# Attention slots that also fix the order of VectorE, ScalarE and GpSimd

## The chip, the cores and the metric

The kernel runs on one core of a Trainium2 chip. The metric is the device time in microseconds (us) of one execution. PE is TensorE's matmul stream and PEld its weight loads, DVE is VectorE, ACT ScalarE, POOL GpSimd, SP the queue that issues most DMAs.

## What is computed

One layer with three branches over 2048 tokens. The change touches only the first, the forgetting attention with 12 heads of 64 channels:

```
F = cumsum(log_f)                                     # per head
s = einsum('bhqd,bhkd->bhqk', q / 8, k)
s = s + F[query] - F[key];  s = where(key <= query, s, -1e30)
y = softmax(s) @ v;         y_fox = y * silu(gf)
```

The other branches (a state-space layer with a gated unit, an attention into 256 memory tokens), the projections, the gated merge and the final norm are as they were.

## The kernel before

The kernel has three parts. Until about 1587 us the input projections and the other two branches run. From there to about 2842 us the attention runs, with other matmuls mixed in ("fill"). Then the rest of the merge and the output follow. The change is in the middle part alone.

**Tasks and slots.** A task is one head `h` and one block `c` of 512 queries. There are 48: twelve heads with c=3, then with c=2, c=1 and c=0. A task with block c has 4(c+1) slots, one for each block of 128 keys: 16, 12, 8 and 4. In a slot `fox_score` makes the scores of 128 keys by 512 queries with two matmuls into one of two buffers `psA`. ScalarE copies them with a bias into `T` (L749), and VectorE takes the running maximum over keys into `mx` (L757; the first slot L759). The last four slots of a task lie on the causal diagonal: there GpSimd first adds a mask to the copy in `T` (L751), and VectorE takes the maximum from `T` (L753) and not from `psA`, over 512, 384, 256 and 128 columns.

**After the scores.** The rest of a task is put into a table `due` by slot, counted as d from its last score slot, so that it runs under the slots of the next task. At d=2 the maximum is transposed on PE into `psB` and reduced to `nm` (L767), then widened on ScalarE into `xb` (L772). At d=4 PE transposes `xb` into `psM`, which has one buffer ("rows"). Then `fox_exp`, for groups of four key blocks: VectorE adds the negative maximum (L789, two key blocks in one instruction of 1024 columns; L794 on the diagonal), ScalarE takes the exponential (L790, L795), GpSimd adds up the denominator in `acc` (L797, L799). PE multiplies with the values into `psC` from d=9 (`fox_pv`). `fox_den` divides, and `fox_end` multiplies with the gate: VectorE L839, then GpSimd L840 over `oo`. `psB` has one buffer too, for the transposes of `mx`, the denominator and the last transposes.

**Fill.** Per slot 0.67 steps of other work are put behind the scores: first the last input projections (`gen_gl`), then part of the merge (`gen_merge0`). A step is mostly six matmuls into `psF`. This work brings splits of weights in two halves, on GpSimd (L931) and VectorE (L933). Its eight first merge steps, somewhere in c=2, have no matmul.

**What sets the order.** The framework's scheduler orders each engine's instructions by its own timeline, and each engine then runs them in that order. For PE the kernel chains the matmuls (`te`), so that PE's order is that of the source. On the other three engines the scheduler moves an instruction ahead as soon as it takes its inputs for ready.

Of the kernel before, what the change touches and what calls it, by code (L numbers as in the profile page):

```python
# [17 lines left out]
CW = 512  # L18
# [4 lines left out]
DH = 64  # L23
# [24 lines left out]
class Layer:  # L48
# [98 lines left out]
        self.te("matmul", out, a[1], b[0], start=False, stop=last)  # L147

    def te(self, op, *a, **k):

        f = getattr(self.nc.tensor, op)
        if not self.chain:
            return f(*a, **k)  # L153
        with self.tc.issue_after(self.pe.ins) if self.pe else nullcontext():
            self.pe = f(*a, **k)  # L155
# [576 lines left out]

    def fox_score(self, p, u, kt):

        nc, h, c = self.nc, u["h"], u["c"]
# [12 lines left out]
        self.te("matmul", ps[:, w:], kk[:, ks], q[1][:, w:], start=False, stop=True)  # L748
        nc.scalar.activation(t[:, a:], ps[:, a:], AF.Identity, bias=bias)  # L749
        if j >= 0:  # L750
            nc.gpsimd.tensor_add(t[:, a:a + 128], t[:, a:a + 128], self.mask)  # L751
            if kt:
                nc.vector.tensor_max(mx[:, a:], mx[:, a:], t[:, a:])  # L753
            else:
                nc.vector.tensor_copy(mx, t)
        elif kt:
            nc.vector.scalar_tensor_tensor(out=mx, in0=ps, scalar=bias, in1=mx, op0=ALU.add, op1=ALU.max)  # L757
        else:
            nc.vector.tensor_scalar(out=mx, in0=ps, scalar1=bias, scalar2=None, op0=ALU.add)  # L759

    def fox_max(self, p, u):

        pt = self.psB()
        for b in range(4):
            self.te("transpose", pt[:, b * 128:(b + 1) * 128], u["mx"][:, b * 128:(b + 1) * 128], self.ident)
        nm = p.tile([128, 4], F32, tag="nm", name="nm", bufs=2)
        self.nc.vector.reduce_max(nm, pt.rearrange("p (b k) -> p b k", b=4), axis=AX.X, negate=True)  # L767
        self.fox_wide(p, u, nm, 128)

    def fox_wide(self, p, u, x, n):  # L770
        u["x"] = p.tile([128, 4, 128], F32, tag="xb", name="xb", bufs=2)
        self.nc.scalar.activation(u["x"][:, :, :n], x.unsqueeze(2).to_broadcast([128, 4, n]), AF.Copy)  # L772

    def fox_rows(self, u, ps, n):

# [1 line left out]
            self.te("transpose", ps[:n, b * 128:(b + 1) * 128], u["x"][:, b, :n], self.ident)  # L777
        return ps

    def fox_exp(self, p, u, g, i):  # L780

        nc, c = self.nc, u["c"]
        tg = u["T"][g]
        if g == 0 and i == 0:
            u["acc"] = p.tile([128, CW], F32, tag="acc", name="acc", bufs=2)
        acc, m = u["acc"], u["m"]
        if g < c:
            t = tg[:, i:i + 2, :]
            nc.vector.tensor_add(t, m.unsqueeze(1).to_broadcast([128, 2, CW]), t)  # L789
            nc.scalar.activation(t, t, AF.Exp)  # L790
        for e in (i, i + 1):
            t, a = tg[:, e, :], 128 * e if g == c else 0
            if g == c:
                nc.vector.tensor_add(t[:, a:], m[:, a:], t[:, a:])  # L794
                nc.scalar.activation(t[:, a:], t[:, a:], AF.Exp)  # L795
            if g or e:
                nc.gpsimd.tensor_add(acc[:, a:], acc[:, a:], t[:, a:])  # L797
            else:
                nc.gpsimd.tensor_copy(acc, t)  # L799

    def fox_pv(self, u, g):

# [14 lines left out]
    def fox_den(self, p, u):  # L817

        nc, h, c = self.nc, u["h"], u["c"]
        u["gf"] = p.tile([DH, CW], F32, tag="gf", name="gf", bufs=2)  # L820
        nc.sync.dma_start(out=u["gf"], in_=self.s["gf"][h * DH:(h + 1) * DH, c * CW:(c + 1) * CW])
        pd = self.psB()
        for b in range(4):
            self.te("matmul", pd[:, b:b + 1], u["acc"][:, b * 128:(b + 1) * 128], self.ones, start=True, stop=True)
        rd = p.tile([128, 4], F32, tag="rd", name="rd", bufs=2)
        nc.vector.reciprocal(rd, pd[:, 0:4])
        self.fox_wide(p, u, rd, DH)
        o = u["o"] = p.tile([DH, CW], F32, tag="oo", name="oo", bufs=2)
        a = 128 if c == 0 else 0
        if a:  # L830
            nc.gpsimd.memset(o[:, 0:a], 0.0)
        nc.scalar.copy(o[:, a:], u["po"][64:128, a:])
        nc.vector.tensor_add(o, u["po"][0:64, :], o)

    def fox_end(self, p, u):
        nc, h, c = self.nc, u["h"], u["c"]
        rb = self.fox_rows(u, self.psB(), DH)
        gf, o = u["gf"], u["o"]
        nc.vector.scalar_tensor_tensor(out=gf, in0=rb[:DH, :], scalar=0.5, in1=gf, op0=ALU.mult, op1=ALU.mult)  # L839
        nc.gpsimd.tensor_mul(o, o, gf)  # L840
        nc.sync.dma_start(out=self.s["yx"][h * DH:(h + 1) * DH, c * CW:(c + 1) * CW], in_=o)
        self.done += 1

    def gen_fox(self):

        p, self.close_f = self.pool("fox", side="right")
        self.ones = p.tile([128, 1], F32, name="ones")
        self.nc.vector.memset(self.ones, 1.0)  # L850
        seq = [(h, c) for c in range(NC - 1, -1, -1) for h in range(H)]
        ld = {0: self.k0}
        due, slot = {}, 0

        def rows(u):
            u["m"] = self.fox_rows(u, self.psum("M"), 128)

        def run():
            for f in due.pop(slot, ()):
                f()  # L860
        for n, (h, c) in enumerate(seq):
            u = {"h": h, "c": c, "ld": ld.pop(n)}
# [340 lines left out]
```

## Time and profile before

| | us |
|---|---|
| median of 3 runs | 3224.64 (3223.2 to 3231.12) |
| profiled execution | 3224.58, span 3222.4 |
| busy in the span: PE / DVE / POOL / ACT | 2998.0 / 1942.0 / 1104.7 / 1035.0 |
| attention, 1587 to 2842: PE / DVE / POOL / ACT of 1255 | 1072.45 / 876.37 / 838.28 / 608.86 |

PE is busy nearly all the time outside of the attention. Inside it PE's own work is dense too, but there are gaps, and the granted clock of PE is 0.92 on the mean. A matmul's end is modelled, so the start of the next one is what tells the pace.

### The profile page before, as it was taken

Reading aid. Unit: us, or ns where it says so; the run is one execution under the profiler, and the core shown is the slowest. Engines: PE = TensorE matmul, PEld = TensorE weight load, DVE = VectorE, ACT = ScalarE, POOL = GpSimd, SP = SyncE. Lnnn points to the kernel's source line nnn. Section 1 sums busy time; section 2 is a strip of 40 time slices with the busy share of each in tenths; the row PEclk is TensorE's granted clock in tenths of the full one; section 3 lists DMA queues with packets and bytes.
Section 4 is the critical chain, followed back from the end, with each engine's and each line's share of the span. In section 5 each row is a group of like instructions: output and inputs, shape, how many; then the busy total and the mean of one; then the engine's idle time right before and its main releaser. Section 6 shows DMA issues by size and latency. Waiting matters only on the chain.

```text
span 3222.4 us, 41372 instructions
## 1 busy us (share of the span) xinstructions
PE 2998.0 (93%) x14096; PEld 2312.9 (72%) x14096; DVE 1942.0 (60%) x3975; ACT 1035.0 (32%) x1840; POOL 1104.7 (34%) x1214
## 2 busy tenths in 40 slices
PE   8999999999999999999988888898788888889999
PEld 7889877777777778888755555566456556667787
DVE  5321589989976643222265555666778887755444
ACT  5112111111122222222255445555445444332222
POOL 0110000000013321221155555566678877722200
PEclk9999999999999999999999888999899998899999
DMA  5342224333346553443533333333456656577543
GB/s 165 111 119 58 72 84 125 106 97 125 127 133 178 165 180 105 129 128 115 150 101 91 91 85 94 96 104 107 135 139 171 197 162 176 176 239 218 172 143 105
DMA packets 283595, 424.90 MB, mean 132 GB/s; under 512 B 108136, under 2 KB 129384, under 8 KB 281848
## 3 DMA queue, kind: packets, MB, share of 16 engines
q1 hardware_dynamic: 283096, 422.19, 44.6%
q8 instruction: 112, 1.84, 0.2%
q14 instruction: 99, 0.81, 0.1%
q10 hardware_dynamic: 288, 0.07, 0.0%
HBM read 287.53 MB, written 134.61 MB: 131 GB/s over the span
## 4 chain that ended last, share of the span: by engine, by line
PE 70%; DVE 11%; DMA 7%; POOL 5%; issue 5%; ACT 2%; SPq 0%; DVEq 0%; POOLq 0%; ACTq 0%
PE psA L153 21%; PE psF L153 20%; PE psF L155 9%; PE psA L155 5%; PE psC L153 4%; PE psC L155 3%; DVE T L789 3%; POOL acc L797 3%; PE psB L153 2%; PE psB L155 2%; DVE T L794 1%; DMA wraw<-in_w_out 1%; DVE mx L753 1%; DVE mx L757 1%; DVE wlo L933 1%
## 5 line engine op out<-in xcount | busy, mean ns | idle before, releaser
L797 POOL TENSOR_TENSOR acc<-acc,T 128x512 f32<-128x512 f32 (+3 forms) x432 | 497.2, 1151 | 23.2 <-ACT T L790 1.5
L749 ACT ACTIVATE T<-psA,nf 128x512 f32<-128x512 f32 x480 | 293.5, 623 | 475.7 <-PE psA L155 444.6
L931 POOL TENSOR_SCALAR whi<-wraw 128x1024 fp32r<-128x1024 f32 (+2 forms) x168 | 168.3, 1002 | 782.5 <-PE psA L153 445.9
L933 DVE TENSOR_TENSOR wlo<-wraw,whi 128x1024 fp32r<-128x1024 f32 (+2 forms) x184 | 232.7, 1266 | 242.6 <-POOL whi L931 215.1
L155 PE MATMUL psA<-qh,kk 128*128 128x512 f32 x480 | 215.7, 450 | 134.1 <-DVE mx L757 124.8
L153 PE MATMUL psA<-hl,whi 128*128 128x512 f32 (+1 forms) x816 | 323.5, 397 | 0.0
L153 PE MATMUL psA<-hh,whi 128*128 128x512 f32 (+1 forms) x816 | 321.4, 395 | 1.7 <-ACT hh L193 1.0
L153 PE MATMUL psA<-hh,wlo 128*128 128x512 f32 (+1 forms) x816 | 322.1, 395 | 0.6 <-DVE wlo L933 0.6
L153 PE MATMUL psF<-hh,whi 128*128 128x512 f32 (+1 forms) x776 | 308.4, 397 | 4.0 <-DVE elo L234 2.5
L153 PE MATMUL psF<-hh,wlo 128*128 128x512 f32 (+1 forms) x776 | 308.1, 397 | 0.1
L153 PE MATMUL psF<-hl,whi 128*128 128x512 f32 (+1 forms) x776 | 308.0, 397 | 0.0
L155 PEld LDWEIGHTS psA<-qh,kk 128*128 128x128 f32 x480 | 96.8, 202 | 240.2 <-DVE mx L757 154.9
L757 DVE SCALAR_TENSOR_TENSOR mx<-psA,nf,mx 128x512 f32<-128x512 f32 x252 | 188.3, 747 | 121.3 <-ACT T L749 115.8
L155 PE MATMUL psC<-T,v 128*64 128x512 f32 (+1 forms) x960 | 212.2, 544 | 0.0
L753 DVE TENSOR_TENSOR mx<-mx,T 128x384 f32<-128x384 f32 (+3 forms) x180 | 145.3, 807 | 100.2 <-POOL T L751 95.8
L155 PE MATMUL psA<-ql,kk 128*128 128x512 f32 x480 | 184.1, 385 | 0.0
L153 PEld LDWEIGHTS psA<-hh,whi 128*128 128x128 f32 x816 | 153.8, 189 | 37.1 <-POOL whi L931 1.8
L153 PEld LDWEIGHTS psA<-hh,wlo 128*128 128x128 f32 x816 | 154.4, 189 | 35.3 <-DVE wlo L933 0.8
L153 PEld LDWEIGHTS psA<-hl,whi 128*128 128x128 f32 x816 | 154.5, 189 | 33.7 <-issue 0.2
L155 PE MATMUL psF<-ymg,whi 128*128 128x512 f32 x512 | 175.8, 427 | 0.0
L153 PEld LDWEIGHTS psF<-hh,whi 128*128 128x128 f32 x776 | 146.6, 189 | 39.0 <-DVE elo L234 3.3
L789 DVE TENSOR_TENSOR T<-psM,T 128x1024 f32<-128x1024 f32 x144 | 166.4, 1216 | 13.0 <-PE psM L155 12.9
(360 smaller groups left out, 6477.2 us busy)
## 6 DMA issues: line engine op xcount, KB each, us to landing
wraw<-in_w_in SPq DMA_DIRECT2D x90, 512.0 KB, 4.0
s_gl<-ehi SPq DMA_DIRECT2D x96, 256.0 KB, 2.4
g<-s_gl SPq DMA_DIRECT2D x96, 256.0 KB, 4.6
wraw<-in_w_proj SPq DMA_DIRECT2D x48, 320.0 KB, 3.4
qh<-s_qh SPq DMA_DIRECT2D x96, 128.0 KB, 4.2
ql<-s_ql SPq DMA_DIRECT2D x96, 128.0 KB, 5.8
wraw<-in_w_glu SPq DMA_DIRECT2D x24, 384.0 KB, 4.6
x<-in_x SPq DMA_DIRECT2D x16, 512.0 KB, 4.5
```

The costliest lines, as they stand in the source:

```text
L153: return f(*a, **k)
L155: self.pe = f(*a, **k)
L749: nc.scalar.activation(t[:, a:], ps[:, a:], AF.Identity, bias=bias)
L753: nc.vector.tensor_max(mx[:, a:], mx[:, a:], t[:, a:])
L757: nc.vector.scalar_tensor_tensor(out=mx, in0=ps, scalar=bias, in1=mx, op0=ALU.add, op1=ALU.max)
L789: nc.vector.tensor_add(t, m.unsqueeze(1).to_broadcast([128, 2, CW]), t)
L794: nc.vector.tensor_add(t[:, a:], m[:, a:], t[:, a:])
L797: nc.gpsimd.tensor_add(acc[:, a:], acc[:, a:], t[:, a:])
L931: self.nc.gpsimd.tensor_scalar(out=hi, in0=x, scalar1=sc, scalar2=1.0, op0=ALU.mult, op1=ALU.mult)
L933: self.nc.vector.tensor_sub(lo, x, fl32(hi))
```

## The change

`te` becomes a case of `ch`, which chains the instructions of any engine in the order of the source, and the attention's instructions on VectorE, ScalarE and GpSimd all go through it (so they carry the one line L159 afterwards). The fill's instructions on these engines stay free. In the table the work of a slot is split into what comes before the score (order 0) and behind it (order 1). The subtractions become `fox_sub`, of which one pair of key blocks is due in every second slot, and the exponentials follow one slot later. The widening (`fox_wide`) and the division's second half (`fox_out`) get slots of their own. At each of the three changes of c four slots without a score are put in; fill runs there too.

```diff
+    def ch(self, eng, op, *a, **k):
+        f = getattr(getattr(self.nc, eng), op)
         if not self.chain:
             return f(*a, **k)
-        with self.tc.issue_after(self.pe.ins) if self.pe else nullcontext():
-            self.pe = f(*a, **k)
+        last = self.last.get(eng)
+        with self.tc.issue_after(last.ins) if last else nullcontext():
+            self.last[eng] = f(*a, **k)
...
-        nc.scalar.activation(t[:, a:], ps[:, a:], AF.Identity, bias=bias)
+        self.ch("scalar", "activation", t[:, a:], ps[:, a:], AF.Identity, bias=bias)
         if j >= 0:
-            nc.gpsimd.tensor_add(t[:, a:a + 128], t[:, a:a + 128], self.mask)
+            self.ch("gpsimd", "tensor_add", t[:, a:a + 128], t[:, a:a + 128], self.mask)
...
+    def fox_sub(self, u, g, i):
+        tg, m = u["T"][g], u["m"]
+        if g < u["c"]:
+            t = tg[:, i:i + 2, :]
+            self.ch("vector", "tensor_add", t, m.unsqueeze(1).to_broadcast([128, 2, CW]), t)
+        else:
+            for e in (i, i + 1):
+                self.ch("vector", "tensor_add", tg[:, e, 128 * e:], m[:, 128 * e:], tg[:, e, 128 * e:])
...
         for n, (h, c) in enumerate(seq):
             u = {"h": h, "c": c, "ld": ld.pop(n)}
+            for _ in range(4 if n and h == 0 else 0):
+                idle()
+                slot += 1
+                yield
             for kt in range(4 * (c + 1)):
-                run()
+                run(0)
                 self.fox_score(p, u, kt)
+                run(1)
...
-            at(1, self.fox_values, p, u)
-            at(2, self.fox_max, p, u)
-            at(4, rows, u)
+            at(1, 1, self.fox_values, p, u)
+            at(2, 1, self.fox_max, p, u)
+            at(3, 1, self.fox_wide, p, u, 128)
+            at(4, 0, rows, u)
             for g in range(c + 1):
                 for i in range(2):
-                    at(4 + 4 * g + 2 * i, self.fox_exp, p, u, g, 2 * i)
-                at(9 + 4 * g, self.fox_pv, u, g)
-            at(11 + 4 * c, self.fox_den, p, u)
-            at(13 + 4 * c, self.fox_end, p, u)
+                    at(4 + 4 * g + 2 * i, 1, self.fox_sub, u, g, 2 * i)
+                    at(5 + 4 * g + 2 * i, 1, self.fox_exp, p, u, g, 2 * i)
+                at(9 + 4 * g, 0, self.fox_pv, u, g)
+            at(11 + 4 * c, 1, self.fox_den, p, u)
+            at(12 + 4 * c, 1, self.fox_out, p, u)
+            at(13 + 4 * c, 1, self.fox_end, p, u)
```

What the table makes of the engines' orders shows at three places. The rows name an instruction by line, operation, output and inputs.

**VectorE, a task with c=3.** Before, from the first score of a task on (`mx<-psA` is the maximum of a score, `T<-psM,T` a subtraction of the task before):

```order
L759 TENSOR_SCALAR mx<-psA,nf 128x512
L767 TENSOR_REDUCE nm<-psB 128x4
L757 SCALAR_TENSOR_TENSOR mx<-psA,nf,mx 128x512 x2
L789 TENSOR_TENSOR T<-psM,T 128x1024 x6
L794 TENSOR_TENSOR T<-psM,T 128x512
L794 TENSOR_TENSOR T<-psM,T 128x384
L794 TENSOR_TENSOR T<-psM,T 128x256
L794 TENSOR_TENSOR T<-psM,T 128x128
L757 SCALAR_TENSOR_TENSOR mx<-psA,nf,mx 128x512
```

Now, over the diagonal of a task and the first two scores of the next one:

```order
L159 TENSOR_TENSOR T<-psM,T 128x1024
L159 TENSOR_TENSOR mx<-mx,T 128x512
L159 TENSOR_TENSOR mx<-mx,T 128x384
L159 TENSOR_TENSOR T<-psM,T 128x1024
L159 TENSOR_TENSOR mx<-mx,T 128x256
L159 TENSOR_TENSOR mx<-mx,T 128x128
L159 TENSOR_TENSOR T<-psM,T 128x512
L159 TENSOR_TENSOR T<-psM,T 128x384
L159 TENSOR_SCALAR mx<-psA,nf 128x512
L159 SCALAR_TENSOR_TENSOR mx<-psA,nf,mx 128x512
```

The ten subtractions of a task no longer stand in one piece between the third and the fourth score, and some of them now stand among the diagonal's maxima.

**GpSimd, a task with c=3.** Before, the masks of a task stand behind all sums of the task before:

```order
L751 TENSOR_TENSOR T<-T,mask 128x128 x4
L931 TENSOR_SCALAR whi<-wraw 128x1024
L799 COPY acc<-T 128x512
L797 TENSOR_TENSOR acc<-acc,T 128x512 x10
L840 TENSOR_TENSOR oo<-oo,gf 64x512
L797 TENSOR_TENSOR acc<-acc,T 128x512 x2
L797 TENSOR_TENSOR acc<-acc,T 128x384
L797 TENSOR_TENSOR acc<-acc,T 128x256
L797 TENSOR_TENSOR acc<-acc,T 128x128
```

Now, from a task's first mask on:

```order
L159 TENSOR_TENSOR T<-T,mask 128x128
L159 TENSOR_TENSOR acc<-acc,T 128x512 x2
L159 TENSOR_TENSOR T<-T,mask 128x128 x2
L159 TENSOR_TENSOR acc<-acc,T 128x512 x2
L159 TENSOR_TENSOR T<-T,mask 128x128
L159 TENSOR_TENSOR acc<-acc,T 128x512
L159 TENSOR_TENSOR acc<-acc,T 128x384
```

The second and third masks now stand behind two sums, and the fourth behind four.

**GpSimd, a task with c=2.** Before:

```order
L799 COPY acc<-T 128x512
L797 TENSOR_TENSOR acc<-acc,T 128x512 x8
L797 TENSOR_TENSOR acc<-acc,T 128x384
L840 TENSOR_TENSOR oo<-oo,gf 64x512
L797 TENSOR_TENSOR acc<-acc,T 128x256
L751 TENSOR_TENSOR T<-T,mask 128x128
```

Now:

```order
L159 TENSOR_TENSOR T<-T,mask 128x128
L159 TENSOR_TENSOR oo<-oo,gf 64x512
L159 TENSOR_TENSOR acc<-acc,T 128x512 x2
L159 TENSOR_TENSOR T<-T,mask 128x128 x2
L159 TENSOR_TENSOR acc<-acc,T 128x512 x2
L159 TENSOR_TENSOR T<-T,mask 128x128
```

With twelve slots the last product of an older task falls on the first diagonal slot, so that `oo` stands ahead of the sums there.

On PE only the places within a slot move (the transposes of `mx` behind the second score and not ahead of it), and no fill is left behind the last task's scores: before, eight steps stood there, which now run in the slots without scores.

More of the change, by code (lines that the diff above doesn't have):

```diff
@@ L793, in fox_exp @@
             if g == c:
-                nc.vector.tensor_add(t[:, a:], m[:, a:], t[:, a:])
-                nc.scalar.activation(t[:, a:], t[:, a:], AF.Exp)
+                self.ch("scalar", "activation", t[:, a:], t[:, a:], AF.Exp)
             if g or e:
-                nc.gpsimd.tensor_add(acc[:, a:], acc[:, a:], t[:, a:])
+                self.ch("gpsimd", "tensor_add", acc[:, a:], acc[:, a:], t[:, a:])
             else:
-                nc.gpsimd.tensor_copy(acc, t)
+                self.ch("gpsimd", "tensor_copy", acc, t)
     def fox_pv(self, u, g):
@@ L825, in fox_den, with fox_out @@
         rd = p.tile([128, 4], F32, tag="rd", name="rd", bufs=2)
-        nc.vector.reciprocal(rd, pd[:, 0:4])
-        self.fox_wide(p, u, rd, DH)
+        self.ch("vector", "reciprocal", rd, pd[:, 0:4])
+        u["n"] = rd
+    def fox_out(self, p, u):
+        c = u["c"]
+        self.fox_wide(p, u, DH)
         o = u["o"] = p.tile([DH, CW], F32, tag="oo", name="oo", bufs=2)
@@ L830, in fox_den @@
         if a:
-            nc.gpsimd.memset(o[:, 0:a], 0.0)
-        nc.scalar.copy(o[:, a:], u["po"][64:128, a:])
-        nc.vector.tensor_add(o, u["po"][0:64, :], o)
+            self.ch("gpsimd", "memset", o[:, 0:a], 0.0)
+        self.ch("scalar", "copy", o[:, a:], u["po"][64:128, a:])
+        self.ch("vector", "tensor_add", o, u["po"][0:64, :], o)
     def fox_end(self, p, u):
@@ L838, in fox_end @@
         gf, o = u["gf"], u["o"]
-        nc.vector.scalar_tensor_tensor(out=gf, in0=rb[:DH, :], scalar=0.5, in1=gf, op0=ALU.mult, op1=ALU.mult)
-        nc.gpsimd.tensor_mul(o, o, gf)
+        self.ch("vector", "scalar_tensor_tensor", out=gf, in0=rb[:DH, :], scalar=0.5, in1=gf, op0=ALU.mult, op1=ALU.mult)
+        self.ch("gpsimd", "tensor_mul", o, o, gf)
         nc.sync.dma_start(out=self.s["yx"][h * DH:(h + 1) * DH, c * CW:(c + 1) * CW], in_=o)
@@ L856, in rows, with run, idle @@
             u["m"] = self.fox_rows(u, self.psum("M"), 128)
-        def run():
-            for f in due.pop(slot, ()):
-                f()
+        def run(order):
+            for f in due.pop((slot, order), ()):
+                f()
+        def idle():
+            run(0)
+            run(1)
         for n, (h, c) in enumerate(seq):
             u = {"h": h, "c": c, "ld": ld.pop(n)}
+            for _ in range(4 if n and h == 0 else 0):
+                idle()
+                slot += 1
+                yield
             for kt in range(4 * (c + 1)):
-                run()
+                run(0)
                 self.fox_score(p, u, kt)
+                run(1)
                 if kt == 1 and n + 1 < len(seq):
@@ L869, in gen_fox @@
                 yield
-            at = lambda d, f, *a: due.setdefault(slot - 1 + d, []).append(lambda: f(*a))
-            at(1, self.fox_values, p, u)
-            at(2, self.fox_max, p, u)
-            at(4, rows, u)
+            at = lambda d, o, f, *a: due.setdefault((slot - 1 + d, o), []).append(lambda: f(*a))
+            at(1, 1, self.fox_values, p, u)
+            at(2, 1, self.fox_max, p, u)
+            at(3, 1, self.fox_wide, p, u, 128)
+            at(4, 0, rows, u)
             for g in range(c + 1):
                 for i in range(2):
-                    at(4 + 4 * g + 2 * i, self.fox_exp, p, u, g, 2 * i)
-                at(9 + 4 * g, self.fox_pv, u, g)
-            at(11 + 4 * c, self.fox_den, p, u)
-            at(13 + 4 * c, self.fox_end, p, u)
+                    at(4 + 4 * g + 2 * i, 1, self.fox_sub, u, g, 2 * i)
[4 more added lines that the diff above has]
+            at(13 + 4 * c, 1, self.fox_end, p, u)
         while due:
-            run()
+            idle()
             slot += 1
@@ L1096, in run @@
         self.chain = self.hi_act = False
-        self.pe, self.done = None, 0
+        self.last, self.done = {}, 0
         self.setup()
```

30 lines of the change are left out of this document (14 added, 16 removed).

## The prediction

> **What bounds the kernel now.** I read the busy time by stages first, then what PE waits for, then the timeline around one wait. The clock for the stages is the moment at which a task's maximum is reduced (L767), once per task. Two rows of the timeline, 11 tasks with c=3 apart:
>
> ```profile
> 1610.72 0.69 DVE L767 TENSOR_REDUCE nm<-psB 128x4 f32<-128x512 f32 x1 [0.36 <-PE psB L155]
> ...
> 2057.38 0.69 DVE L767 TENSOR_REDUCE nm<-psB 128x4 f32<-128x512 f32 x1 [0.29 <-PE psB L155]
> ```
>
> Five windows cut at such moments, with the busy time of PE, PEld, DVE, ACT and POOL, then the granted clock of PE:
>
> ```profile
> 1610.72:2057.38 446.66, 381.78 (x1613) 260.14 (x1612) 261.67 (x343) 226.21 (x347) 255.22 (x245) 0.90 0.34 92
> 2089.52:2254.18 164.66, 148.27 (x705) 101.55 (x704) 111.00 (x152) 93.92 (x150) 106.57 (x108) 1.00 0.41 108
> 2254.18:2435.61 181.43, 147.46 (x622) 96.65 (x620) 138.02 (x181) 83.77 (x136) 127.21 (x129) 0.88 0.53 142
> 2435.61:2664.81 229.20, 198.57 (x940) 136.53 (x939) 203.56 (x258) 106.06 (x188) 195.73 (x201) 0.96 0.61 177
> 2678.64:2807.91 129.27, 114.70 (x582) 86.24 (x581) 97.38 (x158) 54.80 (x120) 97.52 (x135) 0.90 0.61 179
> ```
>
> They are: 11 tasks with c=3 (446.66 / 11 = 40.6 us each), six with c=2 while the last projections fill (27.4), the last six up to c=1, with merge fill (30.2), 11 with c=1 (20.8), 11 with c=0 (11.75). No engine is full in the first two; with c=1 VectorE is busy for 89% and GpSimd for 85%. In c=3 the clock is 0.90, in the second window 1.00.
>
> PE's longest waits in the c=3 stage, and those in c=2 (total, times, longest):
>
> ```profile
> PE psA L155 <- DVE mx L757: 64.9, 15, 6.4
> ...
> PE psA L155 <- DVE mx L757: 15.8, 7, 2.7
> ```
>
> Both name L757, the maximum that holds a score buffer. One task with c=3 (VectorE, then PE) and one with c=2 show why:
>
> ```profile
> 1855.50 6.88 DVE L789 TENSOR_TENSOR T<-psM,T 128x1024 f32<-128x1024 f32 x6 [0.21 <-PE psM L155]
> ...
> 1864.69 0.80 PE L155 MATMUL psA<-qh,kk 128*128 128x512 f32 x1 [5.26 <-DVE mx L757]
> ...
> 2153.86 0.50 PE L155 MATMUL psA<-qh,kk 128*128 128x512 f32 x1 [2.68 <-DVE mx L757]
> ```
>
> Six subtractions run in one piece of 6.88 us. The maximum that frees `psA` stands behind them, so PE idles for 5.26 us. The first matmul after it takes 0.80 us, where the undisturbed ones below take 0.40: the clock is down. In c=2 the same wait is 2.68 us and the clock stays up. So a task with c=3 loses 64.9 / 12 = 5.4 us by waiting and 0.10 x 40.6 = 4.1 us by the clock, and its work on PE is 40.6 - 9.5 = 31.1 us. In c=2 seven waits in six tasks cost 15.8 / 6 = 2.6; the work is 24.8.
>
> **The change, part by part.** It adds and removes no arithmetic; what moves is order.
>
> *The lump goes.* With a subtraction of 1.22 us in every second slot, a score's maximum waits for one of them at most, and PE has two buffers. This ends the 5.4 and 2.6 us above and what they do to the clock. What is late next are the diagonal slots, by the new orders on GpSimd and VectorE. Durations of c=3, where they are least disturbed:
>
> ```profile
> L749 ACT ACTIVATE T<-psA,nf 128x512 f32<-128x512 f32 x134 | 91.1, 688 | 151.3 <-PE psA L155 139.3 <-PE psB L155 11.1
> ...
> L790 ACT ACTIVATE T<-T 128x1024 f32<-128x1024 f32 x66 | 66.1, 1050 | 2.2 <-DVE T L789 1.2
> ...
> L772 ACT ACTIVATE xb<-nm 128x512 f32<-128x512 f32 x11 | 6.8, 621 | 0.0
> ...
> L751 POOL TENSOR_TENSOR T<-T,mask 128x128 f32<-128x128 f32 x40 | 18.6, 473 | 61.1 <-ACT T L749 61.1
> ...
> L797 POOL TENSOR_TENSOR acc<-acc,T 128x512 f32<-128x512 f32 x125 | 163.3, 1307 | 10.2 <-ACT T L790 1.1
> ...
> L840 POOL TENSOR_TENSOR oo<-oo,gf 64x512 f32<-64x512 f32 x10 | 15.6, 1562 | 6.6 <-DVE gf L839 6.6
> ...
> L757 DVE SCALAR_TENSOR_TENSOR mx<-psA,nf,mx 128x512 f32<-128x512 f32 x114 | 85.2, 748 | 74.2 <-ACT T L749 71.6 <-DVE mx L757 0.5
> ...
> L753 DVE TENSOR_TENSOR mx<-mx,T 128x512 f32<-128x512 f32 x10 | 7.8, 779 | 26.5 <-POOL T L751 26.5
> ...
> L753 DVE TENSOR_TENSOR mx<-mx,T 128x384 f32<-128x384 f32 x10 | 6.5, 655 | 6.1 <-POOL T L751 5.8
> ...
> L753 DVE TENSOR_TENSOR mx<-mx,T 128x128 f32<-128x128 f32 x10 | 4.2, 422 | 4.0 <-POOL T L751 3.7
> ...
> L789 DVE TENSOR_TENSOR T<-psM,T 128x1024 f32<-128x1024 f32 x66 | 75.8, 1216 | 3.6 <-PE psM L155 3.6
> ...
> L794 DVE TENSOR_TENSOR T<-psM,T 128x512 f32<-128x512 f32 x11 | 7.5, 682 | 0.0
> ...
> L794 DVE TENSOR_TENSOR T<-psM,T 128x384 f32<-128x384 f32 x11 | 6.0, 550 | 0.0
> ...
> L794 DVE TENSOR_TENSOR T<-psM,T 128x256 f32<-128x256 f32 x11 | 4.6, 417 | 0.0
> ...
> L794 DVE TENSOR_TENSOR T<-psM,T 128x128 f32<-128x128 f32 x11 | 3.1, 283 | 0.0
> ...
> L767 DVE TENSOR_REDUCE nm<-psB 128x4 f32<-128x512 f32 x10 | 6.9, 692 | 9.5 <-PE psB L155 9.5
> ...
> L839 DVE SCALAR_TENSOR_TENSOR gf<-psB,gf 64x512 f32<-64x512 f32 x10 | 6.8, 683 | 8.8 <-PE psB L155 8.8
> ```
>
> And PE's pace, by starts (no stall in between):
>
> ```profile
> 2158.03 0.39 PE L155 MATMUL psF<-hh,whi 128*128 128x512 f32 x1
> ...
> 2159.42 0.40 PE L155 MATMUL psA<-qh,kk 128*128 128x512 f32 x1
> ...
> 2159.89 0.40 PE L155 MATMUL psF<-hh,whi 128*128 128x512 f32 x1
> ...
> 2161.28 0.60 PE L155 MATMUL psB<-ident,xb 128*64 128x128 f32 x4
> ...
> 2161.81 1.94 PE L155 MATMUL psC<-T,v 128*64 128x512 f32 x8
> ...
> 2163.68 0.50 PE L155 MATMUL psA<-qh,kk 128*128 128x512 f32 x1
> ```
>
> Six fill matmuls take 2159.42 - 2158.03 = 1.39 us, a score 0.47, four transposes 0.53, a product with the values 1.87.
>
> *The new chain, c=3.* Time 0 is the end of the first diagonal slot's score. Its copy on ScalarE ends at 0.7, the exponential behind it (1.05) at 1.7, two sums on GpSimd (1.31 each) at 4.4. Only then comes the second mask (0.47): 4.8. VectorE, in order, has waited for it: maximum over 384 columns 5.5, and only then the next subtraction, 6.7. Exponential 7.8, two sums 10.4, the fourth mask 10.9, maximum over 128 columns 11.3. PE now needs that maximum for the transposes of `mx`. It gets there after scores of 384, 256 and 256 columns (0.35 + 0.23 + 0.23, in proportion), a product with the values, two scores and 3.3 fill steps: 0.81 + 1.87 + 0.94 + 4.6 = 8.2 us. It waits for 3.1 us. Then the subtractions of 512 and 384 columns and a maximum (0.68 + 0.55 + 0.75) free the buffer at 13.3, where PE is at 11.3 + 0.53 + 0.9 = 12.7: another 0.6. Then maximum, two small subtractions, reduction and widening (0.75 + 0.42 + 0.28 + 0.69 + 0.62) end at 16.1; PE comes to the transposes into `psM` at 13.3 + 0.47 + 0.9 = 14.7: another 1.4. In all 5.1 us, about as much as the lump cost, but in three pieces. A task then takes 31.1 + 5.1 = 36.2 us if the clock stays up: 11 x (36.2 - 40.6) = -48 us.
>
> *The clock* is the unknown. The trace has gaps of 5.3 us with the clock down, and 2.68 us with the clock up; nothing shows 3.1 us by itself. The ends are no trip at all and one in each task at 4.1 us. By nearness to 2.68 I take one task in four, at half of 4.1, since PE's later two waits swallow the rest: +6. The Trainium skill ("TensorE: Matmul & The Clock Gate", section on HAM oscillation) allows no idle gap on PE longer than about 3.4 us. By that rule 3.1 would cost nothing and this part would be -48; the row of 2.68 agrees with it and the row of 5.26 too.
>
> *The same chain, c=2.* Here the product of an older task stands ahead of the two sums: its gate multiplication on VectorE (0.68) waits for the first mask and the maximum over 512 columns (0.69 + 0.47 + 0.78 + 0.68 = 2.6), the product ends at 4.2, and the rest is 2.5 us later than in c=3: 13.8 at the transposes of `mx`. PE is there after 0.53 + 0.81 + 1.87 + 0.94 and four steps, 5.6: 9.7. It waits for 4.1, then for 1.5 and 0.9 as above: 6.5, against 2.6 before. 6 x (24.8 + 6.5 - 27.4) = +23 us. With a gap of 4.1 I take a trip in every second task, at 1.7 us: +5. By the Trainium skill's 3.4 us (same page and section) each task here would trip and none in c=3: 10 for the +5 and 0 for the +6, so 3214; that lies inside my forecast and is no rival of its own.
>
> *Last six tasks of c=2.* They had 30.2 us each at a clock of 0.88. The chain would make 31 to 33 of them by the fill's own splits on GpSimd, and 12% of 181 is to be had from the clock: 0, with ends of -20 and +20.
>
> *c=1.* The sums of the first exponential are shorter there, and the chain from its first diagonal score over the widened maximum is 16.8 us by the same rows; with transposes, product, two scores and a fill step of PE behind it, 4.2, and 0.5 for splits that fall into it, a task takes 21.5: 11 x 0.7 = +8. The ends are -10, if the splits all fall into idle time, and +30, if they add 2 us more.
>
> *c=0.* Each slot is a diagonal one, and the loop over masks, maxima, subtractions, exponentials and sums closes after four slots. The rows add up to about 11 us with the fill, against 11.75: -6. The last four tasks lose their fill, which ran in the slots without scores; those take 8 x 1.39 = 11 us, and the bare tasks save some 8: together -3, with ends of -15 and +15. The drain of the last task is bare too: before, eight fill steps stood in its waits; now its waits are open, but the steps have been done already. 0, with -5 and +10.
>
> *DMAs.* No load or store is moved to another slot, and PE never waited for one in these windows; nothing.
>
> The sum: -48 + 6 + 23 + 5 + 0 + 8 - 3 = -9, on the profiled execution's 3224.58; the median of the runs, 3224.64, is the same for this purpose. About 3215 us.
>
> **The rivals.** A measurement of this kernel can tell some 0.3% (10 us) from no change.
>
> *The chain doesn't bind.* If GpSimd keeps up on the diagonal, PE's waits go: c=3 at 32.1 (-94 us), c=2 at 25.5 (-11), the rest by a clock near 1 (-15): about 3105. For it speaks that every engine but PE has 40% of its time free in the first two windows; against it, that GpSimd's two sums and VectorE's maximum follow each other in the new orders with no way around. The Trainium skill ("TensorE: Matmul & The Clock Gate", section on the array's architecture) calls the queues of VectorE, ScalarE and GpSimd strictly first in, first out; in the rows above L757 waits behind L789, which agrees.
>
> *Slower: the clock gate goes on tripping.* If every gap of 3 to 4 us brings the clock down at the full 4.1 us, c=3 is at 40.3 and gains 3 us, c=2 is at 35.4 (+48), the next six lose 10 and c=1 8: about 3285. It decides from about one trip in three of these 17 tasks.
>
> *Nothing changes*, because the scheduler's old order was as good: the waits only change places. 3225.
>
> **How the numbers follow.** My forecast, with its own range of 3185 to 3245: 0.4, of which 0.18 is faster than 0.3%, 0.14 the same, 0.08 slower. The chain doesn't bind: 0.25, all faster. The gate: 0.3, of which 0.28 slower, 0.02 the same. Nothing: 0.05, of which 0.04 the same and 0.01 slower. So faster 0.43, same 0.2, slower 0.37. The range of 3130 to 3290 leaves out the better half of the first rival and the tail of the second.
>
> **What the profile would show.** The lump's wait on L757 would be gone, c=3 tasks near 36 us apart, c=2 near 31, c=1 near 21.5, c=0 near 11. PE's waits would stand at the transposes of `mx` (3 and 4 us), VectorE's ahead of the diagonal's maxima for GpSimd's masks, and the clock in c=3 above 0.95. I am wrong if GpSimd's masks start within a slot of their scores; if the clock in c=3 is still near 0.90; or if c=1 and c=0, where VectorE and GpSimd are near full, run at 23 and 13 us by waits of the fixed order.

## The result and the profile after

The changed kernel takes 3402.24 us (3396.53 to 3409.83, 4 runs), the kernel before beside it 3227.88: 5.4% slower, ratio 1.0541 with an interval of 1.0513 to 1.0570. The forecast was 3215 us, with a range that ended at 3290. The profiled execution has a span of 3394.7 us, 172.3 more than before, and all of it lies in the attention.

The same five stages as before, cut at the same tasks. Columns: length, busy time of PE, PEld, DVE, ACT and POOL, then the granted clock of PE:

```profile
1609.30:2039.60 430.30, 372.78 (x1605) 242.35 (x1604) 249.28 (x342) 221.53 (x345) 248.97 (x242) 0.94 0.36 97
2080.24:2275.80 195.56, 161.28 (x698) 104.76 (x696) 106.40 (x151) 92.48 (x151) 106.00 (x108) 0.92 0.34 90
2275.80:2493.49 217.69, 154.36 (x640) 97.80 (x640) 137.22 (x188) 82.23 (x134) 135.86 (x141) 0.82 0.44 124
2493.49:2776.75 283.26, 209.71 (x917) 140.33 (x916) 175.51 (x256) 104.50 (x186) 178.95 (x193) 0.90 0.50 142
2802.20:2989.95 187.75, 124.36 (x535) 94.15 (x534) 89.75 (x158) 55.03 (x120) 93.87 (x128) 0.77 0.41 123
```

Against the rows of before, 11 tasks with c=3 went from 446.66 to 430.30 us, and all later stages grew: 164.66 to 195.56, 181.43 to 217.69, 229.20 to 283.26, 129.27 to 187.75. PE's busy time rose by 7 to 13 us in each of these four, as the clock fell: 1.00 to 0.92, 0.88 to 0.82, 0.96 to 0.90, 0.90 to 0.77. The rest of the growth is time in which PE does nothing.

What PE waits for in the whole attention (total, times, longest), first before, then after:

```profile
PE psA L155 <- DVE mx L757: 124.8, 37, 6.4
```

```profile
PE psC L159 <- ACT T L159: 140.6, 37, 8.8
PE psB L159 <- DVE nm L159: 53.5, 10, 6.8
PE psB L159 <- DVE gf L159: 44.1, 23, 5.7
PE psM L159 <- ACT xb L159: 43.4, 34, 3.3
...
PE psA L159 <- DVE mx L159: 8.2, 6, 1.9
```

The wait that the lump caused fell from 124.8 to 8.2 us. In its place stands a wait that the kernel before did not have: PE holds a product with the values (`psC`) because the exponentials in `T` aren't there, 37 times, up to 8.8 us. The other engines' longest waits name the same chain, from all their waits in that window:

```profile
ACT T L159 <- DVE T L159: 335.3, 126, 10.1
DVE mx L159 <- POOL T L159: 305.3, 122, 4.8
POOL acc L159 <- ACT T L159: 288.9, 141, 10.1
```

ScalarE's exponentials wait for subtractions, VectorE's maxima for GpSimd's masks, GpSimd's sums for exponentials. The diagonal of one task with c=3 shows how this closes; the rows are of all engines, in order of their starts:

```profile
1867.52 0.46 POOL L159 TENSOR_TENSOR T<-T,mask 128x128 f32<-128x128 f32 x1 [0.80 <-ACT T L159]
...
1868.46 2.72 POOL L159 TENSOR_TENSOR acc<-acc,T 128x512 f32<-128x512 f32 x2 [0.49 <-ACT T L159]
...
1869.23 0.28 PE L159 MATMUL psA<-qh,kk 128*128 128x256 f32 x1
...
1869.56 1.08 PE L159 MATMUL psC<-T,v 128*64 128x512 f32 x4
...
1871.14 0.86 POOL L159 TENSOR_TENSOR T<-T,mask 128x128 f32<-128x128 f32 x2
...
1871.62 0.79 DVE L159 TENSOR_TENSOR mx<-mx,T 128x384 f32<-128x384 f32 x1 [2.93 <-POOL T L159]
...
1872.34 1.21 DVE L159 TENSOR_TENSOR T<-psM,T 128x1024 f32<-128x1024 f32 x1
...
1873.59 1.06 ACT L159 ACTIVATE T<-T 128x1024 f32<-128x1024 f32 x1 [3.79 <-DVE T L159]
...
1874.55 0.35 ACT L159 ACTIVATE T<-psA,nf 128x128 f32<-128x128 f32 x1
...
1874.69 1.97 PE L159 MATMUL psC<-T,v 128*64 128x512 f32 x4 [4.05 <-ACT T L159]
1874.79 2.61 POOL L159 TENSOR_TENSOR acc<-acc,T 128x512 f32<-128x512 f32 x2 [2.78 <-ACT T L159]
...
1876.60 0.80 PE L159 MATMUL psA<-qh,kk 128*128 128x512 f32 x1
...
1877.36 0.46 POOL L159 TENSOR_TENSOR T<-T,mask 128x128 f32<-128x128 f32 x1
```

The first mask is done at 1868.0. Then GpSimd takes the two sums that its order has next (2.72 us), and the second and third mask start only at 1871.14, though both scores had been copied by 1869.8. The maximum over 384 columns starts at 1871.62, behind it the subtraction, and behind that the exponential, which ends at 1874.65. PE has done four of the eight matmuls of a product by 1870.64; the other four need just this exponential, so PE idles for 4.05 us. The score of the fourth diagonal slot was made from 1869.23 on, ahead of the product, but its copy (1874.55) stands behind the exponential on ScalarE, and its mask (1877.36) behind two more sums on GpSimd. The chain is a ring: sums, mask, maximum, subtraction, exponential, and again sums. PE isn't part of it here: what stands behind its product is the first score of the next task (1876.60, at half clock, 0.80 us instead of 0.40), which needs no mask.

With c=0 PE stops at another place. Rows of GpSimd, VectorE, PE and ScalarE:

```profile
2865.69 0.62 POOL L957 TENSOR_SCALAR ymg<-yr 128x512 fp32r<-128x512 f32 x1 [2.65 <-DMA yr<-s_ys]
2866.27 0.99 POOL L159 TENSOR_TENSOR acc<-acc,T 128x384 f32<-128x384 f32 x1
...
2867.22 1.31 POOL L159 TENSOR_TENSOR T<-T,mask 128x128 f32<-128x128 f32 x2
...
2868.16 0.79 DVE L159 TENSOR_TENSOR mx<-mx,T 128x384 f32<-128x384 f32 x1 [0.35 <-POOL T L159]
...
2869.40 0.67 DVE L159 TENSOR_REDUCE nm<-psB 128x4 f32<-128x512 f32 x1
...
2870.22 1.84 PE L159 MATMUL psB<-ones,acc 128*128 128x1 f32 x8 [6.80 <-DVE nm L159]
...
2872.67 0.56 PE L159 MATMUL psA<-qh,kk 128*128 128x256 f32 x1
...
2873.48 0.37 ACT L159 ACTIVATE T<-psA,nf 128x128 f32<-128x128 f32 x1 [2.69 <-PE psA L159]
...
2873.93 0.46 POOL L159 TENSOR_TENSOR T<-T,mask 128x128 f32<-128x128 f32 x1 [2.68 <-ACT T L159]
```

GpSimd's first instruction here is a split of the fill, which waits 2.65 us for its load; a sum, two masks, VectorE's maximum and the reduction `nm` stand behind it, and PE's denominator, which needs the one buffer `psB`, waits 6.80 us. Behind the denominator, in PE's order, stands the score of the last slot (2872.67), for which ScalarE's copy and then GpSimd's mask have waited. So with c=0 PE is part of the ring: mask, maximum, `nm`, denominator, score, copy, and again mask. All of the 53.5 us that PE waits for `nm` lie in this stage, and none of its waits for exponentials does.

### The profile page after: what moved, and what is told of

The parts are those of the page before. It is cut to its first block, busy times and chain, and to the rows that moved or that the text cites. A ratio compares the mean times of both kernels' runs of the same rounds, so it can differ in the third digit from the quotient of the medians.

```text
span 3394.7 us, 41337 instructions
## 1 busy us (share of the span) xinstructions
PE 3043.1 (90%) x14096; PEld 2317.3 (68%) x14096; DVE 1883.8 (55%) x3975; ACT 1028.3 (30%) x1840; POOL 1088.4 (32%) x1214
## 4 chain that ended last, share of the span: by engine, by line
PE 63%; POOL 11%; DVE 8%; DMA 6%; ACT 5%; issue 5%; SPq 0%; POOLq 0%; DVEq 0%; ACTq 0%
PE psA L156 20%; PE psF L156 19%; POOL acc L159 7%; PE psF L159 6%; ACT T L159 4%; PE psC L156 3%; PE psA L159 3%; PE psC L159 3%; DVE T L159 2%; PE psB L156 2%; DVE mx L159 2%; PE psB L159 1%; POOL T L159 1%; DMA wraw<-in_w_out 1%; PE psM L159 1%
## 5 line engine op out<-in xcount | busy, mean ns | idle before, releaser
L159 POOL TENSOR_TENSOR acc<-acc,T 128x512 f32<-128x512 f32 (+3 forms) x432 | 500.8, 1159 | 195.5 <-ACT T L159 177.9
L159 ACT ACTIVATE T<-psA,nf 128x512 f32<-128x512 f32 x480 | 292.4, 619 | 441.3 <-PE psA L159 381.4
L159 PE MATMUL psC<-T,v 128*64 128x512 f32 x960 | 247.4, 604 | 140.6 <-ACT T L159 140.6
L159 ACT ACTIVATE T<-T 128x1024 f32<-128x1024 f32 (+2 forms) x336 | 231.3, 716 | 337.9 <-DVE T L159 335.3
L159 DVE SCALAR_TENSOR_TENSOR mx<-psA,nf,mx 128x512 f32<-128x512 f32 x252 | 188.4, 748 | 175.3 <-ACT T L159 174.3
L159 DVE TENSOR_TENSOR mx<-mx,T 128x384 f32<-128x384 f32 (+3 forms) x180 | 103.7, 576 | 290.0 <-POOL T L159 289.8
L159 DVE TENSOR_TENSOR T<-psM,T 128x1024 f32<-128x1024 f32 (+2 forms) x336 | 258.5, 793 | 4.4 <-PE psM L159 4.4
L159 PEld LDWEIGHTS psC<-T,v 128*64 128x64 f32 x960 | 69.8, 145 | 254.5 <-ACT T L159 183.2
L159 PE MATMUL psA<-qh,kk 128*128 128x512 f32 x480 | 212.0, 442 | 19.6 <-ACT T L159 10.5
L159 PEld LDWEIGHTS psA<-qh,kk 128*128 128x128 f32 x480 | 96.9, 202 | 134.6 <-issue 48.8
L159 PE MATMUL psF<-ymg,whi 128*128 128x512 f32 x512 | 187.7, 451 | 0.0
L159 PE MATMUL psA<-ql,kk 128*128 128x512 f32 x480 | 185.3, 387 | 0.0
```

The costliest lines, as they stand in the source:

```text
L159: self.last[eng] = f(*a, **k)
```

## The experiments

Theory A: the fixed orders close a ring on the diagonal, by two links. Link 1 is on GpSimd, where a mask stands behind the sums of the last exponential (A1: this link alone matters); link 2 on VectorE, where a subtraction stands behind a maximum that waits for its mask (A2: VectorE's order alone matters). Rival B: the spread itself and the empty slots cost the time. Rival D: the fill's splits in GpSimd's queue do.

Stage times of all runs, in us. They are cut like the rows above, at the reductions to `nm`; "borders" are the two intervals from c=3 to c=2 and from c=1 to c=0, in which empty slots lie; the third border lies in the last six of c=2. Runs with one time (all but the first two and the last two kernels) stand beside a kernel before that took 3225 to 3233 us. The times are medians, the stages those of the one profiled execution; that of the last row was the slowest of its five, 3182.5 us. The five executions of the last kernel lie 15 us apart (3167.74 to 3182.5), so for a single time a difference of this size is not clear of noise.

| kernel | time | c=3 (11) | c=2, fill (6) | c=2, last six | c=1 (11) | c=0 (11) | borders |
|---|---|---|---|---|---|---|---|
| before | 3227.9 | 446.7 | 164.7 | 181.4 | 229.2 | 129.3 | 46.0 |
| changed | 3402.2 | 430.3 | 195.6 | 217.7 | 283.3 | 187.8 | 66.1 |
| spread only | 3252.4 | 446.4 | 183.5 | 194.9 | 223.0 | 125.7 | 57.0 |
| GpSimd free | 3304.7 | 410.6 | 184.3 | 204.2 | 267.0 | 157.6 | 62.6 |
| sums later | 3289.1 | 412.9 | 180.2 | 203.5 | 257.4 | 158.8 | 60.3 |
| products later | 3409.9 | 431.8 | 192.7 | 215.0 | 314.7 | 167.4 | 65.7 |
| masks on VectorE | 3282.4 | 415.8 | 174.2 | 199.8 | 261.4 | 148.8 | 62.1 |
| splits on ScalarE | 3385.6 | 421.7 | 197.1 | 214.7 | 283.9 | 183.7 | 65.6 |
| subtractions first | 3294.8 | 395.4 | 172.2 | 206.5 | 254.3 | 182.3 | 61.2 |
| both | 3207.4 | 398.7 | 155.4 | 196.2 | 235.8 | 145.3 | 58.5 |
| both, two empty slots | 3221.9 | 399.1 | 165.0 | 187.8 | 243.1 | 152.5 | 50.6 |
| c=3 only | 3198.0 | 413.1 | 168.1 | 181.9 | 228.9 | 130.3 | 49.2 |
| c=3 and c=2, two empty | 3179.2 | 399.3 | 165.0 | 184.0 | 221.3 | 138.1 | 48.7 |
| c=3 and c=2, four empty | 3173.8 | 399.8 | 155.5 | 190.4 | 225.2 | 137.3 | 50.0 |

**Spread only.** The order of the three engines is left to the scheduler again:

```diff
-        if not self.chain:
+        if not self.chain or eng not in ('tensor',):
             return f(*a, **k)
```

> The changed kernel with its slot table, its spread and its four slots without a score, but with VectorE, ScalarE and GpSimd left to the scheduler again; only PE's order is fixed. Theory A (the fixed orders make each diagonal exponential wait for mask, maximum and subtraction in a ring, and PE's product waits for it): the wait of PE at psC on T (140.6 us in the changed kernel) falls below 30 us, and the time comes to 3200 to 3260 us. Rival B (the spread and the empty slots are what costs; the orders only show it): about 3400 us, with the same wait at psC.

It took 3252.38 us: the fixed orders cost 150 us, the spread and the empty slots 25. The product's wait is gone from PE's list, and the old one is back. All waits on a maximum, and VectorE's subtractions of one task:

```profile
PE psA L159 <- DVE mx L156: 128.4, 41, 8.2
```

```profile
1851.54 8.46 DVE L156 TENSOR_TENSOR T<-psM,T 128x1024 f32<-128x1024 f32 x10
```

The scheduler puts all ten subtractions into one piece again, of 8.46 us; the split into slots in the source does nothing for c=3 without the fixed order. Theory A holds against B; the 25 us lie in c=2 (183.5 and 194.9 against 164.7 and 181.4) and at the borders.

**GpSimd free, and sums later.** Two ways to open link 1. The first frees GpSimd alone (the tuple above is `('tensor', 'vector', 'scalar')`). The second keeps all orders, but takes the sums out of `fox_exp` into a `fox_sum` of their own:

```diff
+                    at(6 + 4 * g + 2 * i, 1, self.fox_sum, u, g, 2 * i)
```

> The changed kernel with only GpSimd left to the scheduler; VectorE and ScalarE keep the fixed order. Theory A1 (the ring closes over GpSimd, where the second mask stands behind two sums): masks run ahead of the sums, psC waits fall below 40 us, 3230 to 3290 us. Rival A2 (VectorE's order alone closes it, with the maximum ahead of the subtraction): VectorE still waits for ScalarE's copies and masks, and the time stays at 3370 to 3400 us.

> The changed kernel, all four orders fixed, but the sums of each exponential are issued one slot later, so that on GpSimd a slot's mask stands ahead of the sums of the exponential of the slot before. Theory A1 (mask behind sums closes the ring): VectorE's wait on the masks (305 us) falls by half or more, psC waits below 40 us, 3230 to 3300 us. Rival A2 or B: 3370 to 3400 us, as the changed kernel.

3304.71 and 3289.12 us, 98 and 113 below the changed kernel, so link 1 is real. But the first time lies above the range of theory A1 (3230 to 3290), and in neither run did the product's wait fall below 40 us, which A1 had expected: it is 84.0 and 79.9. From the second run, PE and VectorE:

```profile
PE psC L159 <- ACT T L159: 79.9, 34, 7.3
```

```profile
DVE mx L159 <- POOL T L159: 149.1, 137, 4.3
```

VectorE's wait on the masks halved, from 305.3 to 149.1, the product's from 140.6 to 79.9. What is left goes by another link.

**Products later.** The product with the values, the denominator and the end of a task two slots later, for c below 3:

```diff
+            L = 2 if c < 3 else 0
...
-                at(9 + 4 * g, 0, self.fox_pv, u, g)
+                at(9 + 4 * g + L, 0, self.fox_pv, u, g)
```

(`fox_den`, `fox_out` and `fox_end` get the same `+ L`.)

> The changed kernel with the products with the values, the denominator and the end of a task two slots later for c=2, c=1 and c=0 (c=3 as it was, since its T buffers leave no room). If what PE loses is a delay (the exponential comes 4 to 8 us after PE asks for it, and two slots more would cover it), the psC waits of c=2 and c=1 (about 105 us) go and the time is about 3290 us; c=3 stays at 39 us a task. If the ring itself sets the pace (mask, maximum, subtraction, exponential and sums follow each other all the time), the waits only move to psA or psB and the time stays within 3370 to 3400 us.

```profile
PE psB L159 <- DVE rd L159: 95.4, 20, 11.1
PE psA L159 <- ACT T L159: 55.1, 33, 7.8
...
PE psC L159 <- ACT T L159: 38.3, 13, 4.1
```

3409.86 us, a little above the range of the second case. The product's wait fell by 102 us, and the waits for the denominator (`rd`) and at `psA` took its place. c=0 gained 20 us and c=1 lost 31. More slack does not help on the whole, which fits a ring that sets the pace and a product that is only where PE meets it. The run alone does not show this: the edit also moves the denominator and the end, which use the one buffer `psB`.

**Masks on VectorE.** GpSimd out of the ring by another way:

```diff
-            self.ch("gpsimd", "tensor_add", t[:, a:a + 128], t[:, a:a + 128], self.mask)
+            self.ch("vector", "tensor_add", t[:, a:a + 128], t[:, a:a + 128], self.mask)
```

> The changed kernel with the diagonal's mask additions on VectorE, ahead of their maxima, and not on GpSimd: the hand-over to GpSimd is out of the ring, all else stands. Theory A1 (GpSimd's sums hold the masks, and so maxima, subtractions and exponentials): like the run with the sums one slot later, 3270 to 3310 us, psC waits about 80 us. Rival A2 (VectorE's own fixed order is what holds, GpSimd only happens to be named): 3360 us or more.

3282.42 us, as theory A1 had it, with 70.6 us of waits at `psC`: it is not VectorE's order alone.

**Splits on ScalarE.** `self.hi_act = True` from the start of the attention on, so that the first half of each of the fill's splits runs on ScalarE:

> The changed kernel with the first half of the fill's splits on ScalarE during the attention and not on GpSimd. Theory D (in c=1 and c=0 part of the loss is that the fill's splits stand in GpSimd's queue, wait there for a load or a weight buffer, and hold the masks behind them): the 532 us of c=1 and c=0 fall by 40 us or more, in all 3330 to 3365 us. Rival: ScalarE takes these waits into its own fixed order, ahead of copies and exponentials: 3390 us or more.

3385.62 us, between the two cases; c=1 and c=0 have 283.9 + 183.7 against 283.3 + 187.8 us. Theory D isn't borne out, but the run doesn't rule it out either, since in c=0 ScalarE waits for the loads instead, ahead of its exponentials:

```profile
ACT ymg L955 <- DMA yr<-s_ys: 13.0, 5, 4.1
```

The 17 us that it gained lie in c=3 (8.6) and at other places; they are hardly clear of noise, and I did not follow them. More is said by the run with both links open, below: there GpSimd still waits 26.0 us in c=1 and c=0 for the loads of the splits (`yr`), against 34.6 in the changed kernel, and yet these two stages are 90 us shorter. So D alone explains little of them; what share it has stays open.

**Subtractions first, alone and with the sums later.** Link 2 is opened by issuing a slot's subtractions ahead of its score, and so ahead of its maximum:

```diff
-                    at(4 + 4 * g + 2 * i, 1, self.fox_sub, u, g, 2 * i)
+                    at(4 + 4 * g + 2 * i, 0, self.fox_sub, u, g, 2 * i)
```

Both links first:

> The changed kernel with the sums one slot later, and each slot's subtractions issued ahead of its score, so that on VectorE a subtraction stands ahead of the slot's maximum, which waits for the mask. Theory A (both links of the ring, mask behind sums and subtraction behind masked maximum, cost): a further 25 to 50 us below the 3289 us of the sums alone, 3240 to 3265 us, psC waits below 30 us. Rival (the second link is idle time anyway): 3280 to 3295 us.

3207.42 us, below the theory's own range: 195 us below the changed kernel. PE waits for exponentials at `psC` for only 4.1 us in all; its longest waits, and the stages with c=3 and c=2 under fill:

```profile
PE psM L159 <- ACT xb L159: 37.0, 32, 4.4
PE psB L159 <- DVE gf L159: 30.1, 20, 4.6
```

```profile
1609.87:2008.53 398.66, 362.65 (x1605) 237.48 (x1604) 268.29 (x342) 218.13 (x344) 252.30 (x241) 0.98 0.38 103
2044.11:2199.52 155.41, 148.97 (x698) 99.48 (x697) 109.25 (x151) 91.85 (x151) 108.25 (x109) 1.00 0.40 112
```

The clock is up with the waits gone: 0.98 and 1.00, against 0.94 and 0.92. Then link 2 alone:

> The changed kernel with one edit: each slot's subtractions are issued ahead of its score, so that on VectorE they stand ahead of the slot's masked maximum; on GpSimd the sums stay ahead of the masks. If the two links of the ring add up (sums later alone took 113 us, both together 195 us), this one alone takes about 80 us: 3310 to 3330 us. If opening either link opens the ring for the most part, about 3260 to 3290 us. If the masks behind the sums hold the maxima all the same (the subtraction of the next slot still stands behind them), 3340 us or more.

```profile
PE psB L159 <- DVE mx L159: 71.6, 33, 4.9
PE psB L159 <- DVE nm L159: 53.6, 11, 7.2
...
PE psC L159 <- ACT T L159: 5.2, 6, 1.9
```

3294.82 us, 107 below the changed kernel, between two of the cases. Sums later took 113, both 195, so the links add up but for 25 us, though not in the same stages. Opening link 2 alone brings c=3 to 395.4 us, all that both give; in c=0, where each slot carries a mask, it brings 187.8 only to 182.3, and there link 1 counts (158.8). The product's wait is down to 5.2 us, and PE waits for the masked maxima themselves.

**Fixed orders for some tasks only.** The fixed orders gain in c=3 and lose in c=1 and c=0. First only tasks with c=3 by them (with sums later), the rest by the table of the kernel before, in free orders and without empty slots. The line that decides (the three engines are chained only while `full` is true):

```diff
+            self.full = c == NC - 1
```

> Only the twelve tasks with c=3 get the spread slots and the fixed orders (with the sums one slot later); tasks with c=2, c=1 and c=0 have the table of the kernel before, free orders and no empty slots. If stages are independent, c=3 keeps its 412 us (447 before) and the rest its time of before: 3185 to 3200 us, faster than before by 1%. If what c=3 gains is given back later (fill and loads stand otherwise at the start of c=2): 3215 to 3235 us.

3198.03 us, as expected; c=2, c=1 and c=0 kept their times of before within 4 us. Then c=3 and c=2 with both links open and two empty slots between them.

> Tasks with c=3 and c=2 by the spread slots and fixed orders, with subtractions ahead of the score and sums one slot later, and two empty slots between c=3 and c=2; tasks with c=1 and c=0 by the table of the kernel before, in free orders. From the stage times of the runs (c=3 398.7 us against 446.7, c=2 357.2 with four empty slots against 358.9, the rest as before): 3170 to 3185 us, 1.4% faster than before. If the order of the fill at the borders costs again what is gained: 3195 us or more.

Five rounds: 3179.17 us against 3225.42, ratio 0.9855, interval 0.9838 to 0.9872.

**The empty slots.** The kernel with both links open, with two empty slots a border in place of four:

> As the run with subtractions ahead and sums later (3207 us), with two empty slots in place of four at each of the three borders. The first tasks behind a border took 7 to 11 us more than the later ones, about 2.2 us for an empty slot, of which 0.93 is fill that has to run anyway: six slots less save 6 x 1.3 = 8 us, 3200 us, if an empty slot costs what it lasts. If it covers waits that come back without it: 3205 to 3215 us.

3221.89 us, outside both cases, though 14.5 us between two single times is not clear of noise. The borders gave back 7.9 us and the last six of c=2, with the third border, 8.4, but c=2 under fill lost 9.6, c=1 7.3 and c=0 7.2. The 9.6 us of c=2 come again in the two kernels below (165.0 and 155.5 us). So the slots are not empty time that can be struck out. My explanation is that their number shifts the fill against the slots of all later tasks; what that shift changes inside a task I did not find. The last run uses it:

> The hybrid (c=3 and c=2 by fixed orders, c=1 and c=0 as before) with four empty slots in place of two between c=3 and c=2. In the run with four empty slots everywhere the tasks of c=2 took 26.0 us while the last projections filled, with two 27.1, and the whole of c=2 357.2 against 361.8 us. If that is the number of empty slots (it moves the fill against the slots of all later tasks), c=2 comes to about 357 us and the time to 3170 to 3177 us. If it belongs to the other orders of c=1 and c=0: 3179 us or more, by the two longer slots.

3173.83 us against 3227.09, ratio 0.9831, interval 0.9812 to 0.9850, and c=2 under fill at 26 us a task (155.5 for six).

The intervals of the last two kernels overlap; both beat the kernel before and the changed one.

## Why the prediction was wrong

Its sum, term by term, against the windows (borders and ends by the differences of their limits):

| term | forecast | measured |
|---|---|---|
| c=3, 11 tasks, with its clock | -42 | -16.4 |
| border to c=2 | 0 | +8.5 |
| c=2 under fill, six | +28 | +30.9 |
| last six of c=2, with a border | 0 | +36.3 |
| c=1, 11 | +8 | +54.1 |
| border to c=0 | 0 | +11.6 |
| c=0, 11 | -3 | +58.5 |
| ahead and behind | 0 | -11.2 |
| sum | -9 | +172.3 |

*Right: the lump and the chain in c=3.* The wait on the maximum went, and the new slots alone don't do it: the run with free orders has the lump again, the run with GpSimd alone free has not (7.1 us of such waits). The chain from mask over sums to the next mask was forecast with its links in the right order, and its price of 5.1 us per task came out at 5.2. PE's waits in the c=3 stage:

```profile
PE psC L159 <- ACT T L159: 34.6, 11, 4.1
PE psM L159 <- ACT xb L159: 13.1, 11, 1.9
PE psA L159 <- ACT T L159: 6.2, 6, 1.5
PE psA L159 <- DVE mx L159: 3.5, 3, 1.3
```

They sum to 57.4 us, 5.2 per task, in three pieces near those of the forecast: 3.1 at `psC`, 1.2 at `psM` and 0.9 at `psA`, where it had 3.1, 1.4 and 0.6. What failed is the place of the first. The forecast let PE run on through "a product with the values", 1.87 us of work, to the transposes of `mx`. That product needs the exponential at the end of the chain, so PE stops there, ahead of the transposes. That this piece has the forecast's size is luck: another instruction waits, for another result.

*Wrong: the clock in c=3, one trip in four tasks.* The clock was 0.94, so (1 - 0.94) x 39.1 = 2.3 us per task instead of 0.5; with 31.1 + 5.2 that makes 38.6 of the 39.1 measured. Nine of the eleven waits at `psC` were followed by a lower clock. The sentence "nothing shows 3.1 us by itself" was wrong: the trace of before has two gaps of 3.2 us, told at the end. Here the second rival, the gate that goes on tripping, came nearer, though it had 3285.

*Right in size, by two errors that cancel: c=2 under fill*, 32.6 us a task against a forecast of 24.8 + 6.5 + 0.8 = 32.1. PE's waits there are 5.7 us a task and not 6.5, again first at `psC` (4.1), and the clock takes (1 - 0.92) x 32.6 = 2.6 and not 0.8; the 1.7 us for a trip behind that 0.8 had no row. With free orders in the same slots this stage is slower than before too (183.5 us), by the lump: PE's waits there are 20.1 us, all on a maximum at `psA`.

*Wrong: c=1 and c=0, and the last tasks of c=2.* This is the step that decided: 36 + 46 + 62 = 144 of the 181 us between forecast and result. The forecast priced the chain at 21.5 us for a task with c=1, let the loop of c=0 close over VectorE, ScalarE and GpSimd alone at about 11, and put the last six of c=2 at 0 (their 36 us hold a border too; with free orders in the same slots this stage grew by 13.5). The tasks of c=1 and c=0 took 25.8 and 17.1 us. That they might "run at 23 and 13 us by waits of the fixed order" stood among what would make the forecast wrong.

For c=0 the runs show what it left out: the way round through PE, from the masked maximum over `nm` and the denominator to the next score, its copy and its mask. PE waits for `nm` for 53.5 of the 63.3 us that it waits in this stage. Sums later alone (link 1) bring this to 20.5, subtractions first alone (link 2) leave it at 52.8, both bring it to 17.3. In c=1 PE waits for exponentials (32.1 us), for `gf` at `psB` (28.9) and for `xb` (10.8); with both links open the first two are 1.1 and 13.6. In the last six of c=2 44.7 of 63.2 us are waits for exponentials. Both links together take back 47.5 us of c=1's 54.1 and 42.5 of c=0's 58.5, so the two links are shown as the cause of most of it. The way through PE is read from the trace and these waits; no run took it away by itself. The clock fell from 0.90 to 0.77 at c=0, but PE's busy time, where this shows, grew by only 9.7 of the 58.5 us (for 47 matmuls fewer).

*Smaller slips.* "40% of its time free" for every engine but PE is a third for VectorE and GpSimd in the second window (111.00 and 106.57 of 164.66 us busy). About 11 us against 11.75 for c=0 makes -8 and not -6. "Nothing" for DMAs holds for PE, but GpSimd's waits for the loads of the splits grew from 6.1 to 34.6 us in c=1 and c=0, as said at theory D.

*Wrong: the empty slots and the tail at 0.* The borders cost 8.5 and 11.6 us, the tail gained 9.7. The forecast had counted 11 us of fill for all of them, inside its -3 for c=0.

*The first rival* (the chain doesn't bind, 3105) was not reached even with both links open: 3207 us, and 36.2 us for a task with c=3, not 32.1. That 36.2 is also the forecast's figure is luck, since it was forecast for another order.

*Open:* with both links open c=1 and c=0 are still at 235.8 and 145.3 us, against 229.2 and 129.3 in the kernel before and 223.0 and 125.7 with free orders in the same slots. PE then waits for the widened rows (`xb`) and at the one buffer `psB`; no run took these away. Nor did any run open the place on ScalarE where the fourth copy stands behind an exponential (1874.55 above).

## What to carry to other kernels

A fixed order on several engines joins their queues into rings: before fixing it, follow each instruction to the one that must be done for it, through every engine, the one that bounds the kernel too, until you are back where you began, and see how many slots the way round takes. Issue first what waits for nothing new (a mask, a subtraction) and last what waits for the newest result (a sum), which here was worth 195 us without any change of the work. And fix orders only where the free order is bad. Of the 1.7% that the last kernel gained, the stage c=3 gave nearly all (446.7 to 399.8 us), while the two stages of c=2 came out even (346.1 and 345.9 us); in c=1 and c=0 the scheduler's own order was better.

## What the runs showed of the hardware

I had taken 2.7 us as a gap that leaves the clock up, from the row of before. In the changed kernel two gaps before the second half of a product, each with the 4 us behind it, show otherwise (idle, work, idle, work):

```profile
1675.07:1677.76 2.69, 0.00 (x1) 0.00 (x1) 2.69 (x4) 1.11 (x2) 1.32 (x1) 1.00 1.06 244
1677.76:1681.76 4.00, 4.00 (x13) 2.21 (x13) 1.07 (x3) 0.89 (x2) 3.04 (x3) 0.57 0.99 249
1755.49:1758.39 2.90, 0.01 (x1) 0.00 (x0) 2.09 (x3) 1.11 (x2) 0.21 (x1) 1.00 0.96 202
1758.39:1762.39 4.00, 4.00 (x18) 2.49 (x18) 0.82 (x3) 0.90 (x2) 2.98 (x3) 1.00 0.93 197
```

After an idle time of 2.69 us the clock in the next 4 us was 0.57; after one of 2.90 us it stayed at 1.00. Of the eight gaps of 2.69 to 2.91 us ahead of a product in the c=3 stage, six had a clock of 0.50 within about 1.5 us of their end and two kept 1.00; the three of 4.05 to 4.08 us had 0.50 at once. The trace of before has two gaps of 3.2 us that the forecast did not use: after one (up to 1901.56) the clock was 0.50 from about 1.5 us on, after the other (up to 2024.15) it was 1.00 for the 2.1 us of work to the next gap. So length alone does not decide in this range, and a forecast should count gaps of 2.7 us and more as trips that may happen. The Trainium skill ("TensorE: Matmul & The Clock Gate", section on HAM oscillation) states the rule as no idle gap longer than about 3.4 us; the gap of 2.69 us was shorter and still brought the clock down, so here the measurement decides.
